# Hybrid decoder layer on one core: order of the first loads, a small fill tile, and one ring of three buffers for the convolution

## The chip, the core and the metric

The kernel runs on one core of a Trainium2 chip as one program. The metric is the time of one execution in device microseconds (us); lower is better. Engines: PE is TensorE's matmul (PEld its weight load, which runs beside it), DVE is VectorE, ACT is ScalarE, POOL is GpSimd, SP is SyncE, which here does nothing but issue DMAs. Each engine runs its own instructions in a fixed order and waits where one needs something that isn't there yet.

## The reference, cut to what matters

One decoder layer over x of 2048 tokens by 1024 channels, all in float32.

```python
proj = h @ w_in                                   # 1024 -> 3608 columns
qa, ka, va, ra, lra, qb, kb, vb, zb, bb, ab = split(proj)
o_a = rms(gla_chunked(qa, ka, va, gates(lra))) * silu(ra)          # 4 heads
qkv = silu(causal_conv(concat(qb, kb, vb), conv_w))                # width 4, per channel
o_b = rms(gdn_chunked(l2(qb), l2(kb), vb, beta, g)) * silu(zb)     # 4 heads, delta rule
x = layer_norm(alpha * x + concat(o_a, o_b) @ w_out)
y = top-1 group, then top-2 of its 8 experts (64 SwiGLU experts in all)
out = layer_norm(alpha * x + y)
```

What the change touches is the projection `h @ w_in`, the causal convolution of width 4 with its silu, the small parameters, and a table of expert slots that is filled with a pad value before the routing writes into it.

## The kernel before, in words

The kernel has a front (about 0 to 1000 us: projection, convolution, both kinds of attention), an output projection with routing (to about 1370 us), the experts (to about 2430 us) and a final norm. Matmuls of the front are made of two parts, hi and lo: a value is copied to fp32r on ACT (hi), and DVE or POOL subtract to get the rest (lo); three matmuls (hi by hi, lo by hi, hi by lo) take the place of one.

`mixer_front` (L323) works through four segments of four 128-token tiles. `project(si)` (L366) loads the segment's x in eight half tiles `xt` of 256 KB (L375, ring of three buffers), turns each by four PE transposes into a PSUM tile `mm` (L378), and writes `xhi` on ACT (L382) and `xlo` on DVE (L383). `mm` has two buffers, and the projection's accumulators use them too. Then come 14 blocks of w_in of 256 to 272 columns: four loads `raw` each (L390, three buffers), `whi` on ACT (L392), `wlo` on DVE and POOL in turns (L393). Six of the blocks are token-major (L401, matmuls L412), eight are channel-major (L434, matmuls L440), two steps of 128 channels per block. Six of these eight, 12 steps in a segment and 48 in all, carry the convolution:

- ACT copies the accumulator into `r`, whose tile has the name `cr`, 515 columns, one buffer (L451, L452); POOL puts the last three columns of the segment before in front of it and saves the new ones (L453, L454);
- DVE multiplies and adds four shifted copies by the taps `cw` into `o`, whose tile has the name `oa`, two buffers (L443, L455, L457 three times);
- ACT writes tanh of `o` into `r` (L459), DVE makes silu of both (L460), and SP stores `o` (L463).

The steps of the two blocks without a convolution copy the accumulator straight into an `oa` tile (L445).

Small things that the front sets up: the identity `ident` (L65), the decay parameters `dtb` and `ea` (L274 to L276), the taps `cw` (L334 to L340: a load of conv_w into a tile named `junk`, one PE transpose into an `mm` tile, one DVE multiply), the norm weights `gg` (L341 to L344), the gate weights `wgk` (L345 to L347). `Routing` (L108) fills the table `tab_d` of 1 MB: POOL writes a tile `pad` of 128 by 2048 (L137) and one DMA on SP stores it (L138). All these loads go through SP's queue.

What sets the order: the program is written as above, and a planner (L1667, `schedule_with_timeline_sim=True`) orders each engine's instructions by a simulated timeline when the program is built; earlier lines go first where several are ready. A tile takes one of its name's buffers and gives it back after its last use; the planner turns this into waits between engines. So an edit at the start can move instructions anywhere in the front.

Of the kernel before, what the change touches and what calls it, by code (L numbers as in the profile page):

```python
# [107 lines left out]
class Routing:  # L108
    def __init__(self, tc, nc, consts, jp, tab_d):
        f = lambda name, shape, dt=F32: consts.tile(shape, dt, name=name)  # L110
        self.tc, self.tab, self.puts = tc, tab_d, []
        self.count = f("count", [128, 128])
        self.iota = self.count[:, :NE]
        self.choice = f("choice", [128, NT, 2, 2], I32)
        self.gates = self.choice[:, :, :, 1].bitcast(F32)
        nc.gpsimd.iota(self.choice[:, :, :, 0], pattern=[[256, NT], [1, 2]], base=0, channel_multiplier=2)
        self.known = f("known", [128, NT, 2])
        self.mine, self.base = f("mine", [128, NT, FIRST, 2], BF16), f("base0", [128, NT, FIRST])
        self.found = f("found", [128, FIRST, 2])
        self.before = f("before", [128, 128], BF16)  # L120
        nc.vector.tensor_scalar(self.before, jp, 0.0, None, op0=OP.is_gt)
        self.ones = f("ones_b", [128, 128], BF16)
        nc.vector.memset(self.ones, 1.0)
        self.carry = [f(f"carry{i}", [128, NE]) for i in range(2)]
        nc.vector.memset(self.carry[0], 0.0)
        self.turn = 0
        self.slots = {}
        with tc.tile_pool(name="padp", bufs=1) as pool:
            ii = pool.tile([128, 128], I32, name="iota_i")
            nc.gpsimd.iota(ii, pattern=[[1, 128]], base=0, channel_multiplier=0)  # L130
            nc.vector.tensor_copy(self.count, ii)
            ki = pool.tile([128, NT, 2], I32, name="known_i")
            nc.gpsimd.iota(ki[:, :, 0], pattern=[[0, NT]], base=0, channel_multiplier=1)
            nc.gpsimd.iota(ki[:, :, 1], pattern=[[128, NT]], base=-2 * S, channel_multiplier=0)
            nc.vector.tensor_copy(self.known, ki)
            pad = pool.tile([128, 2 * S * NE // 128], I32, name="pad")
            nc.gpsimd.memset(pad, PAD)  # L137
            nc.sync.dma_start(flat(tab_d, [[2 * S * NE // 128, 128], [1, 2 * S * NE // 128]]), pad)  # L138

    def token_tile(self, nc, work, ps, lg, t):  # L140

# [114 lines left out]
class Gates:  # L256


    def __init__(self, tc, nc, consts, jp, a_log, dt_bias):
        f = lambda name, shape, dt=F32: consts.tile(shape, dt, name=name)  # L260
        self.le = f("le", [128, 128])
        nc.vector.tensor_scalar(self.le, jp, 0.0, None, op0=OP.is_ge)
        self.gt = f("gt", [128, 128])
        nc.vector.tensor_scalar(self.gt, jp, 0.0, None, op0=OP.is_lt)
        self.ones = f("ones", [128, 128])
        nc.vector.memset(self.ones, 1.0)
        self.raw = f("bbab", [128, NT, 8])
        self.g = f("g_all", [128, NT, 4])
        self.beta = f("beta", [128, NT, 4])
        self.cj = f("cj", [128, NT, 4])  # L270
        self.eps_o = f("eps_o", [128, NT, 4])
        self.eg = f("eg", [128, 3, NT, 4])
        self.dtb, self.ea = f("dtb", [128, 4]), f("ea", [128, 4])
        nc.sync.dma_start(self.dtb, row_bcast(dt_bias, 4))  # L274
        nc.sync.dma_start(self.ea, row_bcast(a_log, 4))
        nc.scalar.activation(self.ea, self.ea, AF.Exp)  # L276

    def segment(self, nc, w, ps, c0, n):
# [44 lines left out]
def mixer_front(tc, nc, gt, scan, ident, x, w_in, conv_w, gla_g, gdn_g, w_gk, b_gk, dr):  # L323


    with ExitStack() as es:
# [5 lines left out]
        ps = es.enter_context(tc.tile_pool(name="p2ps", bufs=1, space=PSUM, reuse_waits="tile"))  # L332

        cw = fix.tile([128, 4, 12], F32, name="cw")  # L334
        cr = work.tile([128, 128], F32, name="junk", bufs=1)[:48, :]
        nc.sync.dma_start(cr, flat(conv_w, [[128, 48], [1, 128]]))
        pc = ps.tile([128, 4, 128], F32, name="mm", bufs=2)
        nc.tensor.transpose(pc[:, 0, :48], cr, ident[:48, :48])
        nc.vector.tensor_scalar(cw.rearrange("p a b -> p (a b)"), pc[:, 0, :48], 0.5, None,
                                op0=OP.mult)  # L340
        gg = fix.tile([128, 2, 128], F32, name="gg")  # L341
        nc.sync.dma_start(gg[:, 0, :], row_bcast(gla_g, 128))
        nc.sync.dma_start(gg[:, 1, :], row_bcast(gdn_g, 128))
        nc.vector.tensor_scalar(gg, gg, 0.5, None, op0=OP.mult)  # L344
        wgk = fix.tile([17, 256], F32, name="wgk")  # L345
        nc.sync.dma_start(wgk[:16, :], w_gk)
        nc.sync.dma_start(wgk[16:17, :], b_gk)  # L347
        lT = [fix.tile([17, 128], F32, name=f"lT{i}") for i in range(2)]
        for t in lT:
            nc.gpsimd.memset(t, 1.0)  # L350
# [15 lines left out]
        def project(si):  # L366
            c0, nch = SEGS[si]
            nt = nch * 128
            xhi = ring.tile([128, KD, 512], F32R, name="xhi", bufs=1)
            xlo = ring.tile([128, KD, 512], F32R, name="xlo", bufs=1)  # L370
            for j in range(nch):
                t = c0 + j
                for h in range(2):
                    xt = ring.tile([128, 512], F32, name="xt", bufs=3)
                    nc.sync.dma_start(xt, x[t * 128:(t + 1) * 128, h * 512:(h + 1) * 512])  # L375
                    p = ps.tile([128, 4, 128], F32, name="mm", bufs=2)
                    for k in range(4):
                        nc.tensor.transpose(p[:, k, :],  # L378
                                            xt[:, k * 128:(k + 1) * 128], ident)
                    hi = xhi[:, 4 * h:4 * h + 4, j * 128:(j + 1) * 128]  # L380
                    lo = xlo[:, 4 * h:4 * h + 4, j * 128:(j + 1) * 128]
                    nc.scalar.activation(hi, p, AF.Copy)  # L382
                    nc.vector.tensor_sub(lo, p, hi.bitcast(F32))  # L383
            for kind, b0, n in blocks:
                hi = ring.tile([128, KD, 272], F32R, name="whi")
                lo = ring.tile([128, KD, 272], F32R, name="wlo")
                for h in range(KD // KW):
                    ks = slice(KW * h, KW * h + KW)
                    raw = ring.tile([128, KW, 272], F32, name="raw", bufs=RB)[:, :, :n]
                    nc.sync.dma_start(raw, flat(w_in, [[IN_COLS, 128], [128 * IN_COLS, KW], [1, n]],  # L390
                                                KW * h * 128 * IN_COLS + b0))
                    nc.scalar.activation(hi[:, ks, :n], raw, AF.Copy)  # L392
                    (nc.gpsimd if h % 2 else nc.vector).tensor_sub(  # L393
                        lo[:, ks, :n], raw, hi[:, ks, :n].bitcast(F32))
                passes = ((xhi, hi), (xlo, hi), (xhi, lo))
                if kind == "tok":
                    token_major(si, c0, nch, b0, n, passes)
                else:
                    channel_major(c0, nch, nt, b0, passes)
# [34 lines left out]
        def channel_major(c0, nch, nt, b0, passes):  # L434
            for s in range(2):
                p = ps.tile([128, 4, 128], F32, name="mm", bufs=2).rearrange("p a b -> p (a b)")[:, :nt]
                m = 0
                for k in range(KD):
                    for xs, ws in passes:
                        nc.tensor.matmul(p, ws[:, k, s * 128:(s + 1) * 128], xs[:, k, :nt],  # L440
                                         start=(m == 0), stop=(m == 3 * KD - 1))
                        m += 1
                o = ring.tile([128, 512], F32, name="oa")[:, :nt]  # L443
                if b0 < C_VA:
                    nc.scalar.activation(o, p, AF.Copy)  # L445
                    dst = flat(dr["aT"], [[512, 128], [128 * 512, nch], [1, 128]],
                               c0 * 128 * 512 + (b0 + s * 128))
                else:
                    b = (b0 - C_QB) // 128 + s
                    bo = 2 * b + 1 if b < 4 else 2 * (b - 4) if b < 8 else b  # L450
                    r = ring.tile([128, 515], F32, name="cr", bufs=1)  # L451
                    nc.scalar.activation(r[:, 3:3 + nt], p, AF.Copy)  # L452
                    nc.gpsimd.tensor_copy(r[:, :3], halo[:, b, :])  # L453
                    nc.gpsimd.tensor_copy(halo[:, b, :], r[:, nt:nt + 3])  # L454
                    nc.vector.tensor_scalar(o, r[:, 0:nt], cw[:, 0, b:b + 1], None, op0=OP.mult)  # L455
                    for w in range(1, 4):
                        nc.vector.scalar_tensor_tensor(o, r[:, w:w + nt], cw[:, w, b:b + 1], o,  # L457
                                                       op0=OP.mult, op1=OP.add)
                    nc.scalar.activation(r[:, :nt], o, AF.Tanh)  # L459
                    nc.vector.scalar_tensor_tensor(o, r[:, :nt], 1.0, o, op0=OP.add, op1=OP.mult)  # L460
                    dst = flat(dr["bT"], [[12 * 128, 128], [128 * 12 * 128, nch], [1, 128]],
                               c0 * 128 * 12 * 128 + bo * 128)
# [1208 lines left out]
```

## Time and profile before

| | us |
|---|---|
| median of three runs | 2557.61 |
| the three runs | 2542.12, 2557.68, 2557.61 |
| the profiled execution, its own time | 2542.03 |
| its span in the profile | 2540.0 |
| PE busy | 2401.4 (95%) |
| DVE busy | 1672.7 (66%) |
| ACT busy | 1114.7 (44%) |
| POOL busy | 794.6 (31%) |

The span is the profiled execution without the 2 us around it. A matmul's end is modelled, so neighbouring matmuls overlap in the rows: the distance between their starts is what one costs. PEclk is the clock that TensorE was granted, as a share of full speed.

### The profile page before, as it was taken

The numbers are of one execution on the slowest core, as the hardware profiler recorded it, in microseconds if no ns is written. First come the engines' busy times: TensorE is split into PE (matmuls) and PEld (weight loads), VectorE is DVE, ScalarE is ACT, GpSimd is POOL, SyncE is SP. The second block draws the span as 40 slices with busy tenths as digits, with TensorE's granted clock in tenths as the row PEclk, the third lists the DMA queues.
The fourth block names the chain that finished last, engine by engine and source line by source line (L and its number), as shares of the span: only waits on it lengthen the run. The fifth ranks groups of instructions, "written<-read, shape, count | busy, mean of one in ns | idle before, by whom it ended". The sixth has DMA issues, their size and how long they took to land.

```text
span 2540.0 us, 44666 instructions
## 1 busy us (share of the span) xinstructions
PE 2401.4 (95%) x16115; PEld 1794.8 (71%) x16115; DVE 1672.7 (66%) x3814; ACT 1114.7 (44%) x2202; POOL 794.6 (31%) x967
## 2 busy tenths in 40 slices
PE   7999989999999989889998999999989999999978
PEld 6797769887888778778877466766657667666543
DVE  6746884778577865878887366746645667465537
ACT  3435443554464444622222255645544556455422
POOL 5222582234832482274222111211111111121106
PEclk9999999999999999999999999999999999999989
DMA  5466446555654555645364999999999999999978
GB/s 164 127 188 189 121 112 190 183 150 162 215 175 134 162 174 168 208 128 191 112 235 145 401 408 420 372 401 406 406 409 384 409 407 407 398 400 409 403 284 341
DMA packets 268853, 679.33 MB, mean 267 GB/s; under 512 B 44436, under 2 KB 163798, under 8 KB 217302
## 3 DMA queue, kind: packets, MB, share of 16 engines
q1 hardware_dynamic: 252470, 639.04, 68.7%
q0 software_dynamic: 15744, 36.76, 4.1%
q8 instruction: 128, 2.10, 0.3%
q14 instruction: 95, 0.78, 0.1%
q10 hardware_dynamic: 416, 0.66, 0.1%
HBM read 591.91 MB, written 98.08 MB: 272 GB/s over the span
## 4 chain that ended last, share of the span: by engine, by line
PE 50%; DMA 18%; DVE 8%; issue 3%; ACT 3%; POOL 2%; DVEq 0%; SPq 0%; POOLq 0%; ACTq 0%
DMA w<-in_w_experts_dram 16%; PE gu L1354 14%; PE y L919 7%; PE mm L412 6%; PE y L1354 6%; PE mm L440 3%; PE ysum L1605 2%; DVE w L1218 2%; DVE oa L457 1%; PE misc L943 1%; POOL E L690 1%; PE xt L1355 1%; POOL stmp L688 1%; PE e L543 1%; ACT w L1217 1%
## 5 line engine op out<-in xcount | busy, mean ns | idle before, releaser
L1354 PE MATMUL gu<-w,xh 128*128 128x512 f32 (+1 forms) x2144 | 561.0, 495 | 19.3 <-DVE w L1218 9.4
L1218 DVE TENSOR_TENSOR w<-w,w 128x2048 fp32r<-128x2048 f32 x192 | 435.5, 2287 | 153.3 <-ACT w L1217 124.8
L1217 ACT ACTIVATE w<-w 128x2048 fp32r<-128x2048 f32 x192 | 364.5, 1914 | 199.6 <-PE gu L1354 80.5
L1354 PEld LDWEIGHTS gu<-w,xh 128*128 128x128 f32 (+1 forms) x2144 | 284.9, 166 | 229.3 <-issue 145.2
L1454 POOL DMA_INDIRECT y_d<-xg,ids x52 | 94.4, 1816 | 711.4 <-ACT w L1217 309.9
L1354 PE MATMUL y<-w,hh 128*128 128x512 f32 (+1 forms) x1072 | 280.4, 495 | 9.6 <-DVE w L1218 6.4
L412 PE MATMUL mm<-whi,xhi 128*128 128x256 f32 (+2 forms) x768 | 225.9, 294 | 2.4 <-DVE xlo L383 1.1
L440 PE MATMUL mm<-xhi,whi 128*128 128x512 f32 x512 | 210.3, 411 | 18.4 <-ACT cr L452 18.1
L412 PE MATMUL mm<-whi,xlo 128*128 128x256 f32 (+2 forms) x768 | 220.1, 287 | 0.0
L412 PE MATMUL mm<-wlo,xhi 128*128 128x256 f32 (+2 forms) x768 | 219.9, 286 | 0.0
L1354 PEld LDWEIGHTS y<-w,hh 128*128 128x128 f32 (+1 forms) x1072 | 141.1, 166 | 104.7 <-issue 67.3
L393 POOL TENSOR_TENSOR wlo<-raw,whi 128x512 fp32r<-128x512 f32 (+2 forms) x112 | 151.1, 1349 | 203.0 <-ACT whi L392 200.6
L440 PE MATMUL mm<-xlo,whi 128*128 128x512 f32 x512 | 208.3, 407 | 0.0
L392 ACT ACTIVATE whi<-raw 128x512 fp32r<-128x512 f32 (+2 forms) x224 | 132.5, 628 | 169.2 <-DMA raw<-in_w_in_dram 111.1
L440 PE MATMUL mm<-xhi,wlo 128*128 128x512 f32 x512 | 206.2, 403 | 0.0
L1354 PE MATMUL gu<-w,xl 128*128 128x512 f32 x560 | 176.7, 396 | 0.0
L393 DVE TENSOR_TENSOR wlo<-raw,whi 128x512 fp32r<-128x512 f32 (+2 forms) x112 | 103.0, 926 | 98.0 <-ACT whi L392 96.5
L412 PEld LDWEIGHTS mm<-whi,xhi 128*128 128x128 f32 x768 | 146.1, 190 | 7.5 <-DVE xlo L383 1.5
L412 PEld LDWEIGHTS mm<-whi,xlo 128*128 128x128 f32 x768 | 145.9, 190 | 2.3 <-issue 1.2
L412 PEld LDWEIGHTS mm<-wlo,xhi 128*128 128x128 f32 x768 | 146.1, 190 | 1.0 <-issue 0.2
L1451 DVE SCALAR_TENSOR_TENSOR xg<-y,gate,xg 128x512 f32<-128x512 f32 x104 | 74.6, 746 | 93.3 <-PE y L1354 93.0
L457 DVE SCALAR_TENSOR_TENSOR oa<-cr,cw,oa 128x512 f32<-128x512 f32 x144 | 131.6, 914 | 3.2
(461 smaller groups left out, 4623.8 us busy)
## 6 DMA issues: line engine op xcount, KB each, us to landing
w<-in_w_experts_dram SPq DMA_DIRECT2D x384, 1024.0 KB, 21.5
raw<-in_w_in_dram SPq DMA_DIRECT2D x192, 256.0 KB, 3.1
y<-y_d SPq DMA_DIRECT2D x16, 1024.0 KB, 18.3
bT_d<-oa SPq DMA_DIRECT2D x48, 256.0 KB, 2.4
bT<-bT_d SPq DMA_DIRECT2D x16, 768.0 KB, 5.6
xt<-in_x_dram SPq DMA_DIRECT2D x32, 256.0 KB, 4.0
qk<-bT_d SPq DMA_DIRECT2D x16, 512.0 KB, 4.2
x<-in_x_dram SPq DMA_DIRECT2D x16, 512.0 KB, 4.0
```

Source lines behind the costliest of these rows:

```text
L392: nc.scalar.activation(hi[:, ks, :n], raw, AF.Copy)
L393: (nc.gpsimd if h % 2 else nc.vector).tensor_sub(lo[:, ks, :n], raw, hi[:, ks, :n].bitcast(F32))
L412: nc.tensor.matmul(p[:, :n], xs[:, k, j * 128:(j + 1) * 128], ws[:, k, :n], start=(m == 0), stop=(m == 3 * KD - 1))
L440: nc.tensor.matmul(p, ws[:, k, s * 128:(s + 1) * 128], xs[:, k, :nt], start=(m == 0), stop=(m == 3 * KD - 1))
L457: nc.vector.scalar_tensor_tensor(o, r[:, w:w + nt], cw[:, w, b:b + 1], o, op0=OP.mult, op1=OP.add)
L919: nc.tensor.matmul(pf, a[:, k, :], w[:, k, cs], start=(m == 0), stop=(m == 3 * KD - 1))
L1217: self.nc.scalar.activation(full(hi), full(raw), AF.Copy)
L1218: self.nc.vector.tensor_sub(full(lo), full(raw), full(hi).bitcast(F32))
L1354: mm = lambda *args, **kw: tc.keep_in_program_order(nc.tensor.matmul(*args, **kw))
L1451: nc.vector.scalar_tensor_tensor(yt[:, cs], py[j], col.gate[:, c:c + 1], yt[:, cs], op0=OP.mult, op1=OP.add)
L1454: put = nc.gpsimd.indirect_dma_start(out=y_d, out_offset=bass.IndirectOffsetOnAxis(ap=col.ids[r, c:c + 1], axis=0), in_=yt[r], in_offset=N ...
L1605: keep(nc.tensor.matmul(p[:, cs], ident, ys[t][:, i, cs], start=(i == 0), stop=(i == 1)))
```

## The change

- The pad tile shrinks to 128 by 512, is written by DVE, has a pool of its own at the other side of the memory, and one DMA on ScalarE's queue stores it four times over into the 1 MB table.
- The loads of `dtb`, `ea`, `gg` (two), `wgk` (two) and conv_w move from SP's queue to ScalarE's.
- The taps are made by a function `taps()`, called in the first segment between its first and its second block of w_in, and no longer ahead of the loop.
- `o` and `r` share the name `oa`: three buffers of 515 columns, where there were two `oa` of 512 and one `cr` of 515.

```diff
@@ Routing.__init__
-            pad = pool.tile([128, 2 * S * NE // 128], I32, name="pad")
-            nc.gpsimd.memset(pad, PAD)
-            nc.sync.dma_start(flat(tab_d, [[2 * S * NE // 128, 128], [1, 2 * S * NE // 128]]), pad)
+        with tc.tile_pool(name="padr", bufs=1, side="right") as pool:
+            per = 2 * S * NE // 128
+            pad = pool.tile([128, 512], I32, name="pad")
+            nc.vector.memset(pad, PAD)
+            nc.scalar.dma_start(flat(tab_d, [[per, 128], [512, per // 512], [1, 512]]),
+                                pad[:, None, :].to_broadcast([128, per // 512, 512]))
@@ Gates.__init__
-        nc.sync.dma_start(self.dtb, row_bcast(dt_bias, 4))
-        nc.sync.dma_start(self.ea, row_bcast(a_log, 4))
+        nc.scalar.dma_start(self.dtb, row_bcast(dt_bias, 4))
+        nc.scalar.dma_start(self.ea, row_bcast(a_log, 4))
@@ mixer_front
         cw = fix.tile([128, 4, 12], F32, name="cw")
-        cr = work.tile([128, 128], F32, name="junk", bufs=1)[:48, :]
-        nc.sync.dma_start(cr, flat(conv_w, [[128, 48], [1, 128]]))
-        pc = ps.tile([128, 4, 128], F32, name="mm", bufs=2)
-        nc.tensor.transpose(pc[:, 0, :48], cr, ident[:48, :48])
-        nc.vector.tensor_scalar(cw.rearrange("p a b -> p (a b)"), pc[:, 0, :48], 0.5, None,
-                                op0=OP.mult)
+
+        def taps():
+            cr = work.tile([128, 128], F32, name="junk", bufs=1)[:48, :]
+            nc.scalar.dma_start(cr, flat(conv_w, [[128, 48], [1, 128]]))
+            pc = ps.tile([128, 4, 128], F32, name="mm", bufs=2)
+            nc.tensor.transpose(pc[:, 0, :48], cr, ident[:48, :48])
+            nc.vector.tensor_scalar(cw.rearrange("p a b -> p (a b)"), pc[:, 0, :48], 0.5, None,
+                                    op0=OP.mult)
+
         gg = fix.tile([128, 2, 128], F32, name="gg")
-        nc.sync.dma_start(gg[:, 0, :], row_bcast(gla_g, 128))
-        nc.sync.dma_start(gg[:, 1, :], row_bcast(gdn_g, 128))
+        nc.scalar.dma_start(gg[:, 0, :], row_bcast(gla_g, 128))
+        nc.scalar.dma_start(gg[:, 1, :], row_bcast(gdn_g, 128))
...
-        nc.sync.dma_start(wgk[:16, :], w_gk)
-        nc.sync.dma_start(wgk[16:17, :], b_gk)
+        nc.scalar.dma_start(wgk[:16, :], w_gk)
+        nc.scalar.dma_start(wgk[16:17, :], b_gk)
@@ project
-            for kind, b0, n in blocks:
+            for i, (kind, b0, n) in enumerate(blocks):
+                if si == 0 and i == 1:
+                    taps()
@@ channel_major
-                o = ring.tile([128, 512], F32, name="oa")[:, :nt]
+                o = ring.tile([128, 515], F32, name="oa", bufs=3)[:, :nt]
...
-                    r = ring.tile([128, 515], F32, name="cr", bufs=1)
+                    r = ring.tile([128, 515], F32, name="oa", bufs=3)
```

## Rows read from the trace of the kernel before

**Rows 1.** The page's busy shares in 40 slices of 63.5 us: TensorE and its granted clock in tenths.

```profile
PE   7999989999999989889998999999989999999978
PEclk9999999999999999999999999999999999999989
```

**Rows 2.** Busy time by stretch: the start, the first blocks, then the four stretches that hold the 12 convolution steps of each segment. Columns: stretch, its length, busy us (instructions) of each engine, granted clock, DMA share, GB/s.

```profile
0.00:22.28 22.28, 8.85 (x33) 6.04 (x33) 14.46 (x27) 9.02 (x15) 21.31 (x61) 1.00 0.73 241
22.28:47.00 24.72, 24.62 (x177) 23.39 (x178) 11.98 (x33) 6.23 (x14) 8.13 (x10) 1.00 0.49 145
47.00:150.00 103.00, 96.80 (x422) 76.92 (x421) 72.13 (x118) 42.32 (x77) 28.05 (x42) 0.98 0.45 129
280.00:390.00 110.00, 95.83 (x409) 74.02 (x408) 90.45 (x143) 43.35 (x89) 80.74 (x121) 0.95 0.41 114
540.00:680.00 140.00, 137.61 (x801) 113.50 (x800) 106.15 (x244) 60.91 (x171) 81.89 (x119) 0.99 0.59 177
800.00:940.00 140.00, 131.35 (x773) 106.42 (x772) 109.99 (x265) 59.58 (x158) 79.06 (x120) 0.98 0.55 158
```

**Rows 3.** SP's issues in order of time. Columns: start, us, engine, line, operation, out<-in, count.

```profile
0.79 0.39 SPq L274 DMA_DIRECT2D dtb<-in_dt_bias_dram  x1
...
3.59 0.42 SPq L138 DMA_DIRECT2D tab_d<-pad  x1
...
4.43 2.27 SPq L375 DMA_DIRECT2D xt<-in_x_dram  x3
```

**Rows 4.** TensorE in the first 23 us, in order of time, with the idle time before an instruction and what ended it.

```profile
9.70 1.97 PE L378 MATMUL mm<-ident,xt 128*128 128x128 f32 x8 [5.17 <-DMA xt<-in_x_dram]
12.28 1.12 PE L378 MATMUL mm<-ident,xt 128*128 128x128 f32 x4 [0.61 <-DVE xlo L383]
...
22.28 0.60 PE L412 MATMUL mm<-whi,xhi 128*128 128x272 f32 x1 [1.10 <-DVE xlo L383]
```

**Rows 5.** VectorE, GpSimd and ScalarE at the start, from the timeline: the fill of the pad tile, the making of the identity, the scaling of the taps and of `gg`, and ScalarE's first work on x.

```profile
1.65 1.80 POOL L137 MEMSET pad<- 128x2048 int32 x1
2.32 1.82 DVE L65 TENSOR_SCALAR ident<-jp 128x128 f32<-128x128 int32 x1
7.06 0.19 DVE L339 TENSOR_SCALAR cw<-mm 128x48 f32<-128x48 f32 x1
7.17 0.28 DVE L344 TENSOR_SCALAR gg<-gg 128x256 f32<-128x256 f32 x1
10.90 0.60 ACT L382 ACTIVATE xhi<-mm 128x512 fp32r<-128x512 f32 x1 [6.78 <-PE mm L378]
```

**Rows 6.** DMA in the first 30 us: the rate in 40 slices of 0.75 us, and the loads of x with count, KB each, median us from issue to landing.

```profile
GB/s 0 0 1 15 40 81 285 414 426 306 165 355 401 389 381 390 364 287 194 147 277 287 270 232 328 372 224 63 295 291 139 234 333 349 69 162 201 81 262 36
xt<-in_x_dram SPq DMA_DIRECT2D x11, 256.0 KB, 3.9
```

**Rows 7.** The copy into `cr` at L452 over the whole run: what ended ScalarE's idle time before it, and who waited for it (us in total, times).

```profile
  DVE oa L460: 18.1, 18
  PEld mm L440: 23.3, 15
  PE mm L440: 18.1, 12
```

**Rows 8.** One convolution step of the first segment, from the timelines of VectorE, ScalarE and GpSimd: from the end of one step's silu (L460) to the end of the next.

```profile
69.29 1.22 DVE L460 SCALAR_TENSOR_TENSOR oa<-cr,oa 128x512 f32<-128x512 f32 x1 [0.78 <-ACT cr L459]
70.63 0.60 ACT L452 ACTIVATE cr<-mm 128x512 f32<-128x512 f32 x1 [1.37 <-DVE oa L460]
71.32 0.50 DVE L455 TENSOR_SCALAR oa<-cr,cw 128x512 f32<-128x512 f32 x1 [0.81 <-ACT cr L452]
71.86 2.32 DVE L457 SCALAR_TENSOR_TENSOR oa<-cr,cw,oa 128x512 f32<-128x512 f32 x3
74.96 0.69 DVE L460 SCALAR_TENSOR_TENSOR oa<-cr,oa 128x512 f32<-128x512 f32 x1 [0.78 <-ACT cr L459]
```

**Rows 9.** Matmuls of L440 at two places: two of them with 23 others between, and two neighbours behind a stall.

```profile
56.35 0.40 PE L440 MATMUL mm<-xlo,whi 128*128 128x512 f32 x1
61.92 0.40 PE L440 MATMUL mm<-xlo,whi 128*128 128x512 f32 x1
...
347.26 0.63 PE L440 MATMUL mm<-xlo,whi 128*128 128x512 f32 x1
347.69 0.63 PE L440 MATMUL mm<-xhi,wlo 128*128 128x512 f32 x1
```

**Rows 10.** The copies of L452 in the first and in the second segment (count, ns min/median/max, first and last start in us), and the stores of L463 with their time from issue to landing.

```profile
L452 ACT ACTIVATE cr<-mm x12: 577/599/604, 56.9 to 134.8; 128x512 f32<-128x512 f32 x12
L452 ACT ACTIVATE cr<-mm x12: 574/597/602, 292.7 to 386.3; 128x512 f32<-128x512 f32 x12
L463 SPq DMA_DIRECT2D bT_d<-oa x48: 359/367/1195, 62.2 to 927.9; - x48
DMA to landing us min/median/max: 2.3/2.5/7.1
```

**Rows 11.** TensorE's matmuls into the PSUM tiles named `p` (two buffers), in order of time: L769 belongs to a chunk of the scan, L616 to the preparation of the chunk behind it.

```profile
474.60 0.49 PE L769 MATMUL p<-r,tt 128*128 128x128 f32 x2
484.43 1.05 PE L769 MATMUL p<-v,at 128*128 128x128 f32 x8
485.70 0.49 PE L616 MATMUL p<-ident,bT 128*128 128x128 f32 x3
```

## Prediction

> **What bounds the kernel now.** I read the page's slices first: TensorE is busy in nine tenths of nearly every slice and its granted clock is near full [rows 1]. So time can be won only where TensorE is idle or slow. The change touches two places of the front, so I read TensorE's busy time by stretch next [rows 2]. It is busy for 8.85 of the first 22.28 us, and for 24.62 of the 24.72 us behind that. So the first projection matmul, at 22.28 us, starts a dense stretch: what comes earlier there should come earlier by the same amount behind it, until a stretch that waits for something else. The four stretches with the convolution leave TensorE idle for 6.2, 14.2, 2.4 and 8.7 us (length less busy), 31.5 us in all, at granted clocks of 0.98, 0.95, 0.99 and 0.98 [rows 2].
>
> What ends the idle time at the start: in the timeline TensorE waits for x's first half tile until 9.70 us [rows 4]. SP asked for it at 4.43 us, behind eight small issues that began at 0.79 us, one of them the 1 MB store of the pad table [rows 3]. ScalarE has no work on x until 10.90 us [rows 5].
>
> What ends it in the convolution: I asked the trace who waited for the copy into `cr` (L452). TensorE did, 18.1 us in 12 stalls, and ScalarE was idle for 18.1 us ahead of 18 of the 48 copies until the silu of the step before (L460) was done [rows 7]. The one `cr` buffer thus makes a loop through DVE and ACT: from the end of L460 at 70.51 to the end of the next at 75.65 is 5.14 us, with the copy in between, 0.81 us in which DVE stands still [rows 8]. TensorE's part of a step is 24 matmuls, 61.92 - 56.35 = 5.57 us [rows 9]. The two are close, so whatever else DVE has to do (its half of `wlo`, the gates) makes the loop the longer. The first segment's steps come every (134.8 - 56.9) / 11 = 7.1 us, the second's every (386.3 - 292.7) / 11 = 8.5 us [rows 10].
>
> **The change part by part.**
>
> *Start.* SP's first issue becomes an x load: 0.79 instead of 4.43 us, 3.64 us earlier [rows 3]. In the kernel before, this load took 9.70 - 4.43 = 5.27 us to reach TensorE, where the median is 3.9 [rows 6]; DMA ran at 285 to 426 GB/s from 4.5 to 7.5 us, about 1.07 MB, the pad store ahead of it. With 3.9 us the first half tile is there at 4.7 us, 5.0 us earlier. The identity, ready at 2.32 + 1.82 = 4.14 [rows 5], is just in time. From the first transposes to the first projection matmul are 22.28 - 9.70 = 12.58 us [rows 4], eight half tiles in a ring of three; I leave that as it is. Gain 5.0 us. Bounds: 2.4 us if the pad's megabyte now runs beside x and takes 2.6 us (1.05 MB at 400 GB/s) from these loads; 8.8 us if the loads no longer hold the transposes up, since eight times the 1.1 us of four transposes [rows 4] is 8.8 instead of 12.58 us. I take 5.0, nearest to the median landing time.
>
> The row shows 1 MB moving just ahead of x; whether it still stands in x's way on another queue no row shows. The Trainium skill, page "DMA: Bandwidth & Descriptors", section "Issuing engines are not separate DMA queues", says that DMAs of all issuing engines end on the same 16 DMA engines and interleave, and that a second issuing engine saves only the issue time. By that rule the start gains 2.4 us and not 5.0, a rival below.
>
> *Issues on ScalarE.* Eight issues of about 0.4 us [rows 3] make 3.4 us on ACT. It is free until x's first transposes, 10.90 us before [rows 5], about 5.9 us after. Hidden, cost 0; without that cover at most 3.4 us. DVE's scaling of `gg` (L344, 7.17 us [rows 5]) stands in DVE's queue ahead of the first `xlo`; if `gg` lands late behind the pad store, `xlo` and all behind it on DVE wait, up to 2.6 us. The end of POOL's 1.80 us pad fill [rows 5] only helps POOL, which is busy for 21.31 of 22.28 us [rows 2]; I count nothing. DVE's fill of a quarter of that tile is under 0.5 us by the same row (1.80 / 4).
>
> *Taps.* A transpose (a quarter of 1.1 us, 0.28 [rows 4]) and a DVE multiply of 0.19 us [rows 5] move in front of the second block, on the shared `mm` buffers. The block behind them waits for that multiply: with the two hand-overs about 0.7 us lost. Bounds: nothing, if the planner puts them where TensorE waits anyway, and 3.9 us, the landing time of a load, if conv_w is late. I take 0.7, nearest to the two rows.
>
> *Convolution.* With three buffers for both, the next step's `r` takes the third one as soon as `o` of this step has its own, so the copy no longer waits for L460, and DVE's loop loses its 0.81 us [rows 8]: 4.3 us against TensorE's 5.57. What is late next: `o` takes the buffer of the `r` before it, free after L460, which DVE itself runs; the second next `r` takes the buffer of the first `o`, free when its store has landed, 0.37 + 2.5 us after L460 [rows 10], while a step is 5.57 us. So the new wait is covered by about 2.7 us; for the slowest store, 7.1 us, it isn't. SP carries the stores behind its `raw` loads as before.
>
> At stake are the 18.1 us of stalls [rows 7] and the clock behind them. After such a stall neighbouring matmuls start 0.43 us apart (347.26 and 347.69) and not 0.23 [rows 9]. The four stretches lose (1 - clock) times length, 2.1 + 5.5 + 1.4 + 2.8 = 11.8 us [rows 2]; by these stalls' share of the idle time, 18.1 / 31.5, that is 6.8 us. Sum 24.9 us at most. Not all comes back: in the second stretch DVE is busy for 90.45 of 110 us and POOL for 80.74 [rows 2], so DVE sets the pace there for some steps. I take two thirds, 16.6 us. Lower bound: nothing, if all of it is hidden.
>
> *The planner.* Every instruction of the front is ordered anew. The four stretches do the same 12 steps and idle between 2.4 and 14.2 us [rows 2]; so a new order can cost or give 11.8 us. I take 0 and keep both ends.
>
> **Sum:** 5.0 + 16.6 - 0.7 = 20.9, about 21 us. From the profiled execution's 2542.0 us that makes 2521 us. The three runs shown have a median of 2557.6, 15.6 us above the profiled one, and nothing in the change should move that gap: 2557.6 - 21 is 2537 us, my forecast. Ends: a gain of 8.8 + 24.9 + 11.8 = 45.5, or a loss of 11.8 + 3.9 + 2.6 - 2.4 = 15.9 us.
>
> **Rivals.**
>
> 1. *The convolution's wait was hidden, or the third buffer brings no spare one.* TensorE's stalls go to the next late thing (DVE's gates, the scan), and only the start stays: 5.0 - 0.7 = 4.3 us, 2553 us. For it: DVE at 82% in the second stretch, where TensorE idles most [rows 2]. Against: 12 stalls end on this very copy [rows 7].
> 2. *The pad's megabyte still stands in x's way*, by the interleaving bound above: 2.4 instead of 5.0 us, a gain of 18.3 and 2539 us. For it: DMA moved 241 GB/s on average up to 22.28 us [rows 2], with little room. Against: x is asked for first.
> 3. *Slower: buffers go by the order in which the tiles are named.* The text names `o` ahead of `r`. If buffers were dealt in that order, each `r` would get the buffer of the `o` before it and wait for its store: 0.37 + 2.5 = 2.9 us more in the loop [rows 10], 8.0 us a step against 5.57. Where the loop decides now, 18 steps, that costs 52 us, at all 48 steps 139; between them 95 us, 2653 us. It decides as soon as the store lands later than the copy could start. For it: PSUM tiles of one name are taken strictly in program order. The preparation's L616 starts only when the scan chunk ahead of it has taken its last tile, 1.27 us after that L769 (484.43 to 485.70 [rows 11]). Against: `r` is written first (L452) and `o` only from it (L455), and a tile can be taken no later than its first write.
>
> **How the numbers follow.** Forecast 0.55 (its own range 2518 to 2552, the planner's 11.8 us included), rival 1 0.25, rival 2 0.08, rival 3 0.07, and 0.05 for a new order that eats the gain and more. The range must also hold the chance that the measured runs lie at the profiled execution's level, 15.6 us lower: 2510 to 2563 us leaves out rival 3, the worst orders, and the best tenth. About 1%, 26 us, is what a measurement of this kernel can tell from no change. Faster by over 1% (below 2532 us) is the better part of the forecast and of the lower level, 0.34. Slower by over 1% is rival 3 and a part of the last case, 0.09. The rest, 0.57, is within 1%.
>
> **What would show it.** Right: first L378 at about 4.7 us and first L412 at about 17.3 us; the copy of L452 (under whatever name) no longer waits for L460, TensorE's waits for it fall from 18.1 us to under 6; the first segment's steps come every 6.3 us or less; the second stretch's granted clock rises above 0.95. Wrong: L452 waits for a DMA store (rival 3), TensorE's idle time in the four stretches stays near 31 us under other names (rival 1), or the first L412 comes later than 19 us (rival 2). The stretches behind the front should only shift.

## Result and profile after

The changed kernel takes 2580.9 us (median of four runs, 2578.5 to 2587.1) against 2555.7 us for the kernel before on the same chip: ratio 1.011, 95% interval 1.0074 to 1.0145. It is slower by about 25 us, where 21 us less were forecast. The profiled run took 2587.1 us, its span is 2585.1 us, its mean granted clock 0.961 (0.980 in the profiled run of before).

The page's slices of after, TensorE and its granted clock, beside [rows 1]: the busy shares differ little, but the clock has a 7 and four 8s in the first 23 slices, where before has nines throughout.

```profile
PE   7998989999999988889999999999999999999978
PEclk9999989899999999789999899999999999999989
```

The stretches of [rows 2], the first cut at the first projection matmul (L420, L412 before). Columns as there.

```profile
0.00:23.53 23.53, 8.51 (x32) 5.85 (x33) 13.20 (x27) 8.49 (x14) 19.01 (x60) 1.00 0.71 220
23.53:47.00 23.47, 23.03 (x158) 21.90 (x158) 12.22 (x32) 6.91 (x14) 8.54 (x10) 1.00 0.50 149
47.00:150.00 103.00, 102.69 (x483) 83.96 (x482) 73.44 (x123) 42.95 (x80) 33.67 (x43) 1.00 0.51 148
280.00:390.00 110.00, 97.30 (x412) 76.29 (x411) 86.96 (x136) 36.35 (x74) 81.75 (x117) 0.94 0.44 124
540.00:680.00 140.00, 137.18 (x839) 114.06 (x839) 104.73 (x266) 59.47 (x171) 79.66 (x113) 0.99 0.57 170
800.00:940.00 140.00, 135.96 (x996) 110.93 (x995) 105.00 (x292) 64.53 (x205) 68.08 (x98) 0.96 0.53 157
```

TensorE is idle for 0.3, 12.7, 2.8 and 4.0 us in the four stretches, 19.9 us against 31.5 before. The convolution did get faster. The copy, now L460, over the whole run (beside [rows 7]): what ended ScalarE's idle time before it, and who waited for it.

```profile
  PE mm L448: 1.8, 2
  PEld mm L448: 15.7, 7
  PE mm L448: 13.0, 7
```

Its times in the first and second segment (beside [rows 10]):

```profile
L460 ACT ACTIVATE oa<-mm x12: 572/579/583, 59.3 to 127.4; 128x512 f32<-128x512 f32 x12
L460 ACT ACTIVATE oa<-mm x12: 573/578/597, 289.5 to 375.7; 128x512 f32<-128x512 f32 x12
```

A matmul, 1.8 us, is all that the copy itself waits for: the 18.1 us of waits for the silu are gone. TensorE still waits for the copy, 13.0 us in 7 stalls (18.1 in 12 before). The first segment's steps come every (127.4 - 59.3) / 11 = 6.2 us (7.1 before), the second's every 7.8 (8.5).

Of the 13.0 us, 12.7 lie in the second segment, where it was 4.2 before (who waited for the copy there, before and then after):

```profile
  PE mm L440: 4.2, 6
```

```profile
  PE mm L448: 12.7, 6
```

ScalarE's timeline ahead of one of these stalls, then TensorE's row:

```profile
322.40 0.63 ACT L467 ACTIVATE oa<-oa 128x512 f32<-128x512 f32 x1 [4.37 <-DVE oa L465]
322.94 0.58 ACT L460 ACTIVATE oa<-mm 128x512 f32<-128x512 f32 x1
```

```profile
323.57 0.50 PE L448 MATMUL mm<-xhi,whi 128*128 128x512 f32 x1 [3.10 <-ACT oa L460]
```

The copy no longer waits for a buffer, but in ScalarE's order it stands behind the tanh of the step before (L467), and that waited 4.37 us for VectorE's tap sums (L465). In five of the six stalls the tanh ahead of the copy had waited 4.4 to 5.2 us for VectorE. So VectorE still holds up the copy there, by another way.

The start, beside [rows 3, 4]: SP's issues, then TensorE, then what SP's queue waited for in the first 30 us (us in total, times, longest).

```profile
0.81 4.77 SPq L381 DMA_DIRECT2D xt<-in_x_dram  x3
7.60 3.74 SPq L398 DMA_DIRECT2D raw<-in_w_in_dram  x3
```

```profile
4.83 1.11 PE L384 MATMUL mm<-ident,xt 128*128 128x128 f32 x4 [4.83 <-DVE ident L65]
10.05 1.11 PE L384 MATMUL mm<-ident,xt 128*128 128x128 f32 x4 [4.11 <-DMA xt<-in_x_dram]
...
23.53 0.60 PE L420 MATMUL mm<-whi,xhi 128*128 128x272 f32 x1
```

```profile
SPq L381 <- DMA dtb<-in_dt_bias_dram: 2.8, 1, 2.8
SPq L398 <- DMA gg<-in_gdn_norm_g_dram: 2.2, 1, 2.2
SPq L398 <- DMA tab_d<-pad: 2.0, 1, 2.0
```

The first half tile is transposed at 4.83 us, as forecast. The second waits until 10.05, and the first projection matmul comes 1.25 us later than before. SP's x load stands still 2.8 us until dt_bias has landed, a load that ScalarE issued and that x does not need. In the compiled program the DMAs of SP and ScalarE take eight completion semaphores in turn, and an engine issues a DMA only when the one before it on its semaphore has landed, whichever of the two engines issued that one. The second x load has dt_bias's semaphore and is issued at 4.00 us. Before, the first x load had it; but that load came at 4.43 us, and dt_bias had landed at 3.36, so nothing was lost.

**Where the time went.** TensorE's time up to the last matmul of the output projection (1377.3 us in a second trace of before, 1401.6 after) is cut where projection matmuls begin and end, and for each piece two things are summed from the views by stretch: idle (length less busy) and clock loss (busy times one less granted clock). The second trace of before (`before_again`, 2550.6 us) is used, since the first is of its fastest run: idle 81.1 and 81.4 us in the two, clock loss 33.4 and 49.6. The clocks in these views have two places, so a sum is good to a microsecond or two. And clock loss overstates what the clock costs: these 16 us go with only 8.5 us of time (2542.0 and 2550.6).

| us idle + clock loss | before again | after |
|---|---|---|
| start, to the first projection matmul | 14.0 + 0 | 15.0 + 0 |
| convolution stretches (with the blocks ahead of them in the first) | 28.4 + 16.0 | 17.2 + 11.0 |
| token-major blocks ("token blocks") behind the convolution | 1.9 + 0 | 15.2 + 5.7 |
| attention and scan between segments, and the tail | 37.1 + 33.6 | 51.1 + 46.9 |
| sum | 81.4 + 49.6 | 98.3 + 63.7 |

The convolution gained 16.2 us by these sums (12.6 against the first trace of before, which has 30.8 + 10.0 there), and 46 us were lost behind it. The sums overstate here too: they differ by 31 us, while the last matmul of the output projection comes 24.3 us later. The two traces differ by 36.5 us in all. The other 12 us lie behind that matmul (1171.3 us before again, 1183.5 after), with a granted clock of 0.92 over its first 148 us, 0.99 before again. The other runs of after are 5 to 9 us faster than this profiled one, so a part of the 12 us may be this run's own.

Most of TensorE's idle time in the token blocks is waits for what empties its PSUM tiles: two copies on ScalarE and a multiply on VectorE, 13.6 us together where it was 1.8 before again.

```profile
PE mm L420 <- ACT st L424: 7.1, 2, 6.8
PE mm L420 <- ACT oa L453: 3.6, 3, 2.8
PE mm L420 <- DVE st L431: 2.9, 1, 2.9
```

Three of the pieces behind the convolution, before again and then after: token blocks of segments 3 and 4, and the stretch to the first output projection.

```profile
666.00:722.00 56.00, 54.13 (x433) 51.39 (x432) 32.17 (x71) 29.61 (x73) 38.75 (x56) 1.00 0.71 212
945.00:997.00 52.00, 52.00 (x460) 49.97 (x459) 20.14 (x54) 21.18 (x56) 18.09 (x28) 1.00 0.52 159
997.00:1108.00 111.00, 94.93 (x1390) 76.38 (x1389) 85.09 (x365) 65.53 (x261) 32.68 (x58) 0.86 0.65 202
```

```profile
663.00:726.00 63.00, 57.28 (x437) 54.15 (x435) 24.22 (x59) 25.64 (x66) 35.00 (x52) 0.95 0.66 196
938.00:1002.00 64.00, 56.79 (x432) 53.44 (x430) 30.15 (x72) 26.00 (x81) 34.80 (x52) 0.95 0.56 172
1002.00:1121.00 119.00, 98.05 (x1436) 78.01 (x1435) 84.05 (x380) 68.27 (x256) 32.47 (x50) 0.81 0.52 166
```

And the cause that I set out to test: the last step of segment 4's gates (a logarithm, Ln, on ScalarE), which the attention of that segment needs, stands at 931.6 us before again and at 1002.9 after, at the end of the token blocks. In segments 2 and 3 it comes 31 and 18 us later than before again.

```profile
931.62 1.06 ACT L482 ACTIVATE E<-E 128x1024 f32<-128x1024 f32 x1
```

```profile
1002.89 1.06 ACT L490 ACTIVATE E<-E 128x1024 f32<-128x1024 f32 x1
```

### The profile page after: what moved, and what is told of

It reads as the page before. It is cut to its first block, busy times and chain, and to the rows that moved or that the text cites. A ratio compares the mean times of both kernels' runs of the same rounds, so it can differ in the third digit from the quotient of the medians.

```text
span 2585.1 us, 44679 instructions
## 1 busy us (share of the span) xinstructions
PE 2430.6 (94%) x16115; PEld 1821.3 (70%) x16115; DVE 1666.1 (64%) x3815; ACT 1113.8 (43%) x2202; POOL 799.0 (31%) x966
## 5 line engine op out<-in xcount | busy, mean ns | idle before, releaser
L420 PE MATMUL mm<-whi,xhi 128*128 128x256 f32 (+2 forms) x768 | 229.5, 299 | 14.2 <-ACT st L424 7.1
L420 PE MATMUL mm<-whi,xlo 128*128 128x256 f32 (+2 forms) x768 | 224.8, 293 | 0.0
L420 PE MATMUL mm<-wlo,xhi 128*128 128x256 f32 (+2 forms) x768 | 224.5, 292 | 0.0
L420 PEld LDWEIGHTS mm<-whi,xhi 128*128 128x128 f32 x768 | 149.7, 195 | 20.6 <-ACT st L424 7.5
L420 PEld LDWEIGHTS mm<-whi,xlo 128*128 128x128 f32 x768 | 149.7, 195 | 2.8 <-issue 1.5
L420 PEld LDWEIGHTS mm<-wlo,xhi 128*128 128x128 f32 x768 | 150.1, 195 | 1.9 <-issue 1.0
L1357 POOL DMA_INDIRECT xg<-x_d,tok x50 | 74.2, 1484 | 188.4 <-DMA y_d<-xg,ids 43.5
```

What stands on the lines that cost most here:

```text
L420: nc.tensor.matmul(p[:, :n], xs[:, k, j * 128:(j + 1) * 128], ws[:, k, :n], start=(m == 0), stop=(m == 3 * KD - 1))
L1357: return nc.gpsimd.indirect_dma_start(out=xg[n % 5][r], out_offset=None, in_=x1_d, in_offset=bass.IndirectOffsetOnAxis(ap=col.tok[r, c:c + ...
```

## Experiments

Theory A: the gates of the next segment stand behind its whole projection in program order. The planner gave them the gaps that the waiting convolution left; with no gaps they move to the projection's end, and the attention behind them starts late, with less for TensorE to do beside it. Theory B: the start's edits cost, through ScalarE's queue and the order that follows. Theory C: `r` and `o` in one ring wait for o's store.

Each ratio is against runs of before on the same chip. The kernels were timed on several chips; before's medians there lie between 2554.3 and 2555.7 us.

**The two halves.** `start_only` is the diff without the two lines on `oa` and `cr`; `conv_only` is those two lines alone.

> The start's edits alone (x's loads first on SyncE, small loads and the table's fill on ScalarE's queue, taps behind the first block); the convolution keeps its two o buffers and one r buffer. Theory A (the loss comes of the convolution's shorter steps: they leave no gaps for the next segment's gates, which come later in the planner's order): the start costs only what its own first matmul shows, +1.3 us; 2557 us, within 2552 to 2562. Theory B (the loss comes of the start's edits: ScalarE's queue holds up SyncE's issues, and the planner's order moves from there on): most of the 25 us stand here already, 2572 to 2585. Theory C (r and o in one ring of three wait for o's store): as A, 2555 to 2559.

> The three shared buffers alone, with the start of before. Theory A: the four convolution stretches sum to about 326 us as after the whole change (356 before), but the gates' Ln of segments 2 to 4 comes 25 us and more later than before, and the time is 2570 to 2585 us. Theory B: the convolution's 16 us and more are kept, 2525 to 2540. Theory C: 2570 to 2585 as in A, with GpSimd's copies of the halo waiting for stores for 30 us or more.

Measured: 2560.7 us, ratio 1.0024 (1.0009 to 1.0039), and 2567.8 us, 1.0045 (1.0025 to 1.0065). Both cost; neither is the whole 25 us, so A's and B's numbers were both too simple: the first is within A's range, the second just under the 2570 of A and C. In `conv_only` segment 4's Ln is at 1000.4 us, in `start_only` at 937.2. C's sign is there as well: in `conv_only` GpSimd's copy of r's three head columns (L453) waits 30.5 us for o's stores, in 11 waits.

**The gates' place.** In the projection of segments 2 to 4 (this edit and those below are shown in short):

```
 for i, (kind, b0, n) in enumerate(blocks):
+    if si and i == 2:
+        segment_gates(si)
...
-segment_gates(si)
+if si == 0:
+    segment_gates(0)
```

> The three shared buffers, the start of before, and the gates of segments 2 to 4 called inside the projection right behind its first two blocks, which give all that they read (ahead of the convolution in the planner's order). Theory A: the gates are done before the convolution ends, the attention of the next segment starts where it did before or sooner, and the convolution's gain shows: 2520 to 2545 us, faster than before. Theory B: no different from the three buffers alone. Theory C: the waits for the stores are as they were, 2570 to 2585.

> The kernel before with the gates of segments 2 to 4 called behind the first two blocks, nothing else changed. Theory A: here the convolution's waits already let the gates in, so the call moves little: 2540 to 2558 us, and the kernel with three buffers and early gates is 10 us or more faster than this one. Theories B and C: 2553 to 2560.

Measured: 2552.3 us, 0.9990 (0.9977 to 1.0003), and 2554.9 us, 0.9994 (0.9973 to 1.0014). The same edit is worth 15.5 us with three buffers and nothing in the kernel before, as A has it. But A's 2520 to 2545 us was missed, and so were the 10 us between the two kernels (2.7 by the medians): early gates bring back what the buffers alone had lost, and the convolution's gain does not show beyond that. It speaks against C that GpSimd's head copy waits longer here than in `conv_only` (34.4 us, 13 waits) in a kernel that is 15.5 us faster. The other direction, and the whole change:

```
-segment_gates(si)
+with tc.issue_after(last_token_matmul.ins):   # segments 3 and 4
+    segment_gates(si)
```

> The kernel before, convolution untouched, with TensorE's part of the gates of segments 3 and 4 forced behind the last matmul of their projection (issue order only). Theory A (late gates are what costs): the Ln of segments 3 and 4 comes near the end of the projection or behind it, the attention of those segments starts that much later, and the time is 2566 to 2580 us, 10 to 25 us over before. Rival (the late gates are only a sign of something else): 2553 to 2560.

> The changed kernel with the gates of segments 2 to 4 called behind the first two blocks of their projection. Theory A: the 12 to 16 us that early gates brought to the three buffers alone come back here too, 2563 to 2570 us (2581 without). If the loss is the planner's order at large and not the gates: 2575 to 2587.

Measured: late 2567.3 us, 1.0034 (1.0016 to 1.0051), with segment 4's Ln at 1005.5 us; after with early gates 2554.7 us, 0.9995 (0.9984 to 1.0006), Ln at 921.4. Late gates alone cost before some 9 to 12 us, and early gates alone take back all the 26 us that the change lost, again with more of C's waits (38.4 us). That is more than the 12 to 16 us that A had forecast, and twice what late gates cost before: either late gates cost more beside the change's other edits, or the call moves more of the order than the gates. No run parts these two. In the sums of the table this kernel has 14.6 + 0 at the start, 14.1 + 6.3 in the convolution, 16.1 + 4.4 in the token blocks and 37.9 + 37.1 in the rest: the rest is back near before's, the convolution gains 24.0 us, and the token blocks keep 18.6 of them.

**The order by chance.** Before once more, and before with two blocks swapped (`C_KA` ahead of `C_QA`, the two channel-major blocks without a convolution).

> The kernel before itself, one run, for a trace near its median: 2545 to 2562 us. The trace of before that stands so far is of its fastest run (2542, granted clock 0.980); here the same order of instructions with a mean granted clock of 0.970 to 0.975 and the same idle time, so that the difference between two runs of one kernel is in the clock.

> The kernel before with two blocks of the projection swapped (the second gated branch's keys ahead of its queries): the same work in the same loops. If an order's chance is small: 2551 to 2559, within 0.2% of before. If the planner's order scatters by itself: off by 5 us or more in either direction.

Measured: 2550.6 us with clock 0.975, and 2554.7 us, 1.0009 (0.9997 to 1.0021). This new order costs nothing, nor did that of `before_gates_early`; a scatter of 25 us by order alone is not seen in these two. Both change little, so they do not exclude a smaller scatter where more is moved.

**The start.** All loads on SyncE's queue. In `start_on_sync` the small loads stand behind x's in program order; in `start_x_first` the order is held:

```
 with tc.issue_after(third_x_load.ins):
     gg's two loads on nc.sync
...
 with tc.issue_after(eighth_x_load.ins):
     taps, dt_bias, a_log, w_gk, b_gk, the table's fill on nc.sync
```

> The kernel before with x's loads first, and all small loads and the table's fill (from a small tile) behind them on SyncE's own queue: gg behind x's first loads, the rest behind the first block of weights; nothing on ScalarE's queue. Theory S (the changed kernel's second x load was held because DMAs of two queues take turns on eight completion semaphores, and an issue waits for the earlier transfer on its semaphore when that is of the other queue): the first three x loads are issued within 2 us, the first projection matmul comes at 17 to 19 us (22.3 before, 23.5 after), 2549 to 2553 us, 2 to 5 us under before. Rival (the small transfers and the x loads fight for the DMA engines whatever the queue): first matmul at 21 us or later, 2553 to 2558.

> The kernel before with all loads on SyncE's queue and the order there held: x's first three loads, then gg, then x's others and the weights in turns, and behind x's eighth load the taps, dt_bias, a_log, w_gk and the table's fill. The last try left the order to the planner, and it put the small loads first again. Theory S (ScalarE's queue and its shared completion semaphores hold x up, not the transfers themselves): the first three x loads are issued by 2 us, the first projection matmul comes at 16 to 19 us, and the time is 2549 to 2553. Rival (the start's order is not what sets the first projection matmul): it comes at 21 us or later, 2553 to 2560.

Measured: 2561.6 us, 1.0016 (0.9995 to 1.0037), and 2552.6 us, 1.0001 (0.9987 to 1.0015). In the first the planner put the seven small loads ahead of x again, and the first projection matmul came at 22.68 us; it says nothing on the queue. In the second, SP and TensorE:

```profile
0.80 1.34 SPq L391 DMA_DIRECT2D xt<-in_x_dram  x3
```

```profile
4.97 1.97 PE L394 MATMUL mm<-ident,xt 128*128 128x128 f32 x8 [4.97 <-DVE ident L65]
...
18.07 0.60 PE L430 MATMUL mm<-whi,xhi 128*128 128x272 f32 x1 [0.36 <-DVE xlo L399]
```

Three x loads in 1.34 us, and the first projection matmul at 18.07, 4.2 us earlier than before. So x's loads ahead of the small ones, on one queue, give nearly the forecast start; they are then among the first eight DMAs and find no semaphore in use. Queue, order and the place of the table's megabyte were changed together, so this does not say that ScalarE's queue was at fault, nor does it part the semaphores from the megabyte: in the changed kernel the second x load was issued at about 4.0 us (0.81 + 0.4 + 2.8), 3.2 us late, and took 6.05 us to TensorE, where 3.9 is the median [rows 6]. Nor do the 4.2 us show in the whole: in its trace the output projection ends at 1372 us, between the 1366 and 1377 of the two traces of before, and by the medians there is no difference.

**The head columns.** GpSimd copies r's three head columns and, in the same queue, makes half of the weights' low parts. With three buffers that copy waits for a store (27.4 us, 11 times, in the changed kernel).

```
-nc.gpsimd.tensor_copy(r[:, :3], halo[:, b, :])
+nc.scalar.activation(r[:, :3], halo[:, b, :], AF.Copy)
```

> Three shared buffers, early gates, and the 3 head columns of r copied by ScalarE, not GpSimd, so that GpSimd no longer waits for o's store in front of the low halves of the weights. Theory C2 (what is left of the convolution's gain is lost in the token blocks behind it, because weight loads wait for GpSimd's low halves: 95 us of such waits in SyncE's queue against 69 before): these waits fall to 75 us or less, TensorE's idle time in the token blocks goes, and the time is 2538 to 2548 us, 5 to 14 under the same kernel with the head on GpSimd (2552). Rival (the chain from convolution to attention and scan bounds the segment, whatever the token blocks do): 2548 to 2556.

> Three shared buffers and r's head columns copied by ScalarE, gates where they were. Theory A with C2 (both late gates and late weight loads cost): some 6 us under the three buffers alone (2568), so 2559 to 2564, still over before by 4 to 9. If the head's copy was all of it: 2550 or less.

> The kernel before with r's three head columns copied by ScalarE, not GpSimd. The r buffer is waited for as before, so the convolution's steps stay as they are; ScalarE gets 48 copies of some 0.2 us, GpSimd loses them. Off the path: 2551 to 2559. If GpSimd's wait in front of the weights' low halves costs in this kernel too: 2545 to 2550.

Measured: with early gates 2546.2 us, 0.9953 (0.9935 to 0.9971); without them 2562.4, 1.0036 (1.0021 to 1.0051); in the kernel before 2566.6, 1.0055 (1.0036 to 1.0075), above both of its ranges. The sign that I had set for C2 failed: SyncE's waits for GpSimd's low halves did not fall to 75 us, they went from 95 to 108, while the time fell by 6. In the kernel before, the copy stands in the loop of the one `r` buffer: the waits of L452 for the silu grew from 18.1 us to 30.9, and the gates came late here too (Ln at 987.6 us).

```profile
  DVE oa L460: 30.9, 22
```

**Together.** Three buffers and early gates throughout.

> Three shared buffers, early gates, and the start with everything on SyncE's queue and x first. If the parts add: the start's 2 to 5 us on top of the 2552 of buffers and early gates, 2546 to 2551. If the planner's order eats the start as it ate others: 2550 to 2560.

> Three shared buffers, early gates, r's head columns on ScalarE, and x first with the held order on SyncE. If the start's gain adds: 2540 to 2544 us, 4 us under the same kernel with the start of before (2546), 11 to 16 under before. If the planner's order eats it, as with the start edits so far (6 us lost each time): 2546 to 2554.

Measured: with the start of `start_on_sync` 2559.1 us, 1.0008 (0.9991 to 1.0025), which is not clear of the same kernel without it (0.9977 to 1.0003); with x first and the head on ScalarE 2536.3 us, 0.9945 (0.9924 to 0.9966), 10 us under `conv_early_head_act` where 4 were forecast. This is the fastest. What do the buffers and the head do in it?

> The fastest kernel so far (2536) with the convolution's two o buffers and one r buffer of before. If the shared buffers bring their 16 us once the gates come early and the start is in order: 2548 to 2556 here. If its gain comes of the rest: 2532 to 2542.

> Three shared buffers, early gates, x first with the held order on SyncE, r's head columns on GpSimd as in both kernels. If the head's place matters with three buffers: 2545 to 2551. If it does not: 2533 to 2542, as with the head on ScalarE.

> The fastest kernel once more (three shared buffers, early gates, x first, head on ScalarE): 2531 to 2543 us if its gain stands, 0.4 to 0.8% under before; 2545 or more if the first runs flattered it.

Measured: with before's two `o` and one `r` 2562.7 us, 1.0038 (1.0022 to 1.0054); with three buffers and the head on GpSimd 2557.3, 1.0008 (0.9991 to 1.0025), both above both of their ranges; the fastest once more 2534.4, 0.9927 (0.9900 to 0.9953). So the three buffers are worth 26 us there (the 12 us that the head on ScalarE cost in a kernel with one `r` may be a part of it; that is not shown), and the head's place 23 us, where it was 6 with the start of before. By the medians x first is worth 10 us with the head on ScalarE and costs 5 with it on GpSimd, though the intervals overlap in both cases. The parts do not add, so the order that comes of each combination has its own share in these numbers. The profiled runs show where the head's 23 us lie: idle in the token blocks 18.6 us with the head on GpSimd, 6.6 in the fastest; clock loss 42.3 and 32.0, a difference smaller than that of the two traces of before. Who waited for L465, the copy of the last channel blocks, with the head on GpSimd, and ScalarE's timeline there:

```profile
  PE mm L432: 11.3, 4
```

```profile
390.15 1.23 ACT L412 ACTIVATE whi<-raw 128x512 fp32r<-128x512 f32 x2 [0.92 <-DMA raw<-in_w_in_dram]
395.06 0.63 ACT L412 ACTIVATE whi<-raw 128x512 fp32r<-128x512 f32 x1 [3.68 <-DMA raw<-in_w_in_dram]
395.60 0.58 ACT L465 ACTIVATE oa<-mm 128x512 f32<-128x512 f32 x1
```

The copy that empties TensorE's PSUM tile runs behind a weight conversion that waited 3.68 us for its load. In the fastest, who waited for the same copy, and what the head copy (L473) waited for:

```profile
  PE mm L432: 1.1, 1
```

```profile
  DMA bT_d<-oa: 59.3, 27
```

ScalarE now waits for o's stores 27 times, 59.3 us, and the kernel is the fastest all the same. Why the planner's ScalarE order turns out better with that copy on it is not settled.

## Why the prediction was wrong

- *Start, "I take 5.0".* The first half tile came as forecast (4.83 against 4.7). The step "Issues on ScalarE ... cost 0" failed: I counted ScalarE's time and not that SP's issues would wait for those loads to land, 2.8 + 2.2 + 2.0 us. The term came out at -1.25 us. With the loads on one queue and the order held it is 4.2 of the 5.0 us. Of rival 2 the sign appeared (first L412 later than 19 us); its megabyte as the only cause is not shown.
- *Taps, 0.7.* TensorE waits 0.4 us for the taps; near enough.
- *Convolution, 16.6.* The mechanism was right for the buffer: the waits of L452 for L460 went from 18.1 us to none, the first segment's steps shortened to 6.2 us, and the convolution stretches gave back 16.2 or 12.6 us of idle time and clock, by the trace of before that is taken. That this lies near 16.6 is in part luck, since "two thirds" was no more than a choice. Left out was ScalarE's own order, with the tanh of the step before ahead of the copy: in the second segment TensorE's waits for the copy rose from 4.2 to 12.7 us. So these waits (13.0, "under 6" forecast) and the second stretch's clock (0.94, "above 0.95" forecast) did not come out.
- *The planner, "I take 0 and keep both ends", 11.8 us.* This is the step that failed. Its bound was read from the convolution stretches, but the edit's effect on the order fell on the work that had lived in their gaps. By the sums of the table, late gates and the tighter token blocks cost 46 us behind them; in time the whole front came out 24 us longer. It is the case to which the prediction gave 0.05, a new order that eats the gain and more. With the gates early, everything else of the change left as it was, the time is that of before (0.9995): the order made the loss, and the gain was still not there.
- *Rival 1* named the gates as what is late next, with nothing lost beside the gain; their delay costs more than the convolution gained.
- *Rival 3* did not come: L460 waits for no store, and the next `r` does not take the buffer of the `o` before it. The buffers go round as the forecast had it, and its "new wait" for the store of the `o` two steps back came as well. But it fell on GpSimd's copy of the head columns, which the prediction did not look at: 27.4 us in 11 waits. Below, that copy waits for a store issued at 85.24 us, while the step between ends its silu only at 89.6.

```profile
87.64 0.55 POOL L461 COPY oa<-halo 128x3 f32<-128x3 f32 x1 [2.36 <-DMA bT_d<-oa]
```

- "Nothing in the change should move that gap": it did move. The profiled run of before was its fastest by clock, 15.6 us under the median, and the second trace has the same idle time; the profiled run of after lies 6.2 us above its median.

What stays open: why `start_only` loses 6 us with a start only 0.9 us later (first projection matmul 23.17), why an earlier start does not show in the time of the kernel before, whether x first on two queues would do as well as on one, where the convolution's gain would show with the gates early and all else of the change as it is, and what the head's place does to ScalarE's order.

## What to carry to other kernels

Where a planner fills waits with other work, a wait that is removed takes that work's place away: look for what ran in the gap, and give it a place of its own (here early gates) together with the edit. A stretch that gets faster must be read with the stretches behind it, idle time and clock loss added up. And where DMAs take a few completion semaphores in turn, a small load ahead in that turn can hold up a large one behind it, from another engine's queue too: put the loads that matter first in the turn. Here x first on one queue gave the start that was wanted.

## What was not expected of the hardware

- Two traces of one kernel differ by 16 us of clock loss (33.4 and 49.6 us) at the same idle time (81.1 and 81.4 us), and by 8.5 us in time (2542.0 and 2550.6): here it is the granted clock, and nothing in the program, that makes the difference.
- In the tail, between segment 4's token blocks and the output projection, TensorE idles most and its granted clock is low: over 111 us with 16 us idle it was 0.86, over 119 us with 21 us idle 0.81, a mean of its levels of 2.4 and 1.2 GHz. In the 56 us of token blocks before, with 2 us idle, it was 1.00. The two do not go in step: the tail of `conv_head_act` has 11 us idle in 112 us and a clock of 0.80, that of `before_head_act` 25 us in 122 and 0.86.
